# Projecting the dilated attention groups in token order instead of residue order, in a two-layer decoder trunk

## The chip, the cores and the metric

The kernel runs on one core of one Trainium2 chip. The metric is the device time of one execution in microseconds (us), as the median of several runs. Five engines work side by side, each through its own list of instructions in order: TensorE (PE; its weight loads are told apart as PEld) multiplies matrices, VectorE (DVE) and ScalarE (ACT) do elementwise work, GpSimd (POOL) does little here, and SyncE (SP) issues every DMA.

## The reference: what is computed

Two layers, each a token mixer and a feed-forward block over 512 tokens of 1024 channels. The part that the change touches is the dilated attention, branch A of the mixer:

```
for g, (window, dilation) in enumerate(((128, 1), (512, 4), (2048, 16))):
    q = apply_partial_rope(qkv_a[:, :, g, 0], cos, sin)
    k = apply_partial_rope(qkv_a[:, :, g, 1], cos, sin)
    o, lse = dilated_causal_attention(q, k, qkv_a[:, :, g, 2], window, dilation)
# alpha = softmax over the three groups of lse;  o_a = sum over groups of alpha * o
```

A query of a group with dilation d attends to keys whose token number has the same remainder modulo d. With 512 tokens and four heads per group, the groups with dilation 4 and 16 both live inside the four residue classes modulo 4, of 128 tokens each. Beside branch A there are a sparse attention with an indexer and a top-128 selection (B), a differential attention (C), sigmoid gates, and a gated convolutional feed-forward.

## The kernel before, in words

All matrix products are done in float32 as three products of a high and a low part (`mm3`, lines L88 to L90: hi*hi, hi*lo, lo*hi). The normalized input stands transposed in SBUF as `xh` and `xl` (128 channels on partitions, 8 channel blocks `KT`, 512 tokens). Weights come in from DRAM by SP into `wr` (two buffers) and are split into `wh` (a cast on ACT, L81) and `wl` (a subtraction on DVE, L82), five buffers each.

The mixer runs through the list `ORDER`: projection units A(g,p), where g is the group and p a pair of heads, the indexer I, then C and B units, and four branch stages (`ga`, `gc`, `gb`) that multiply the gates and the finished attention outputs. One projection unit (`proj_unit`) makes four token tiles of 128; each tile is 24 matmuls with 128 tokens of `xh` or `xl` as the stationary operand and 384 weight columns (q, k and v of two heads) as the moving one, into one of three PSUM banks `mm`. Then ACT copies q and k out (`qr`, L416), ACT and DVE split v into high and low parts straight from PSUM (L81, L82), DVE applies the rotary embedding, and after every second tile PE transposes q and k (L439) into a PSUM bank `tp`, from which ACT and DVE build the stacked operands `qkT` (`double_k`, L395 and L397; `stack_q`, L388 to L391): six reads by ACT and six by DVE for each two tiles.

The groups g = 1 and g = 2 are projected in residue order: tile t takes tokens t, t+4, t+8, ..., so that `xtile` gives a slice with a step of four floats. These are four units in each layer: A(1,0), A(2,0), A(1,1), A(2,1). Every other unit takes 128 neighbouring tokens:

```
if perm:
    return lambda k: (xh[:, k, t::4], xl[:, k, t::4])
return lambda k: (xh[:, k, t * P:(t + 1) * P], xl[:, k, t * P:(t + 1) * P])
```

The attention itself is cut into chains (scores, transposed probabilities, product with v), which `slot()` starts one by one between tiles and branch steps; `later(f, n)` puts f off by n slots. The joint output of groups 1 and 2 goes through DRAM once (`ascr`, L579 and L581) to come back in token order. The order of the instructions on each engine is set by the scheduler of the framework when the program is built, from its own estimates; on the chip each engine then works through its list.

Of the kernel before, what the change touches and what calls it, by code (L numbers as in the profile page):

```python
# [17 lines left out]
P = 128  # L18
# [19 lines left out]
TWO_PI = [6.28125, 0.0019350051879882812, 3.019813448190689e-07]  # L38
TWO_PI_REST = 1.0253376273028358e-11
MAGIC = 12582912.0  # L40
SBUF_SLOTS = dict(u=10, qk=4, v=4, wr=2, wh=5, wl=5, sm=4, pt=4, qr=2, th=3, s=24, s1=2, md=4, wi=1, lp=1, q0=2, cw=1)
PSUM_BANKS = dict(mm=3, sc=2, tp=2, pv=1)

ORDER = [("A", 0, 0), "I", ("A", 1, 0), ("A", 2, 0), ("A", 0, 1), ("A", 1, 1), ("A", 2, 1), ("C", 0), ("C", 1),
# [5 lines left out]
def tile_trunk(ctx, tc, x, positions, w_in, w_br_a, w_br_b, w_br_c, w_out, lam_q1, lam_k1, lam_q2, lam_k2,  # L50
# [10 lines left out]
    def alloc(shape, dtype, tag):  # L61
        uid[0] += 1
        return sb.tile(shape, dtype, tag=tag, name=f"{tag}{uid[0]}", bufs=SBUF_SLOTS[tag])

# [186 lines left out]
    first += [pre_norm(xts[t], t, g_first, xts[t]) for t in range(2, NT)]  # L251
    pos_n = alloc([4, P], I32, "pt")
    nc.sync.dma_start(pos_n, positions[0].rearrange("(t p) -> t p", p=P))
    pos_p = alloc([P, 4], I32, "pt")
    nc.sync.dma_start(pos_p, positions[0].rearrange("(p r) -> p r", r=4))

    cmask = cp.tile([P, S], BF16, name="cmask")
    nc.gpsimd.memset(cmask, 0.0)
# [19 lines left out]

    posf_n = alloc([4, P], F32, "pt")
    nc.vector.tensor_copy(posf_n, pos_n)  # L280
    posf = alloc([P, 8], F32, "pt")
    tpos = palloc("tp")
    nc.tensor.transpose(tpos[:, 0:4], posf_n, ident[0:4, 0:4])
    nc.vector.tensor_copy(posf[:, 0:4], tpos[:, 0:4])
    nc.vector.tensor_copy(posf[:, 4:8], pos_p)
    ang = alloc([P, 8, 8], F32, "th")
    for f in range(8):
        nc.vector.tensor_scalar(ang[:, :, f], posf, INV_FREQ[f], None, op0=ALU.mult)
    rn = alloc([P, 8, 8], F32, "sm")
    rh = alloc([P, 8, 8], F32, "sm")  # L290
    rl = alloc([P, 8, 8], F32, "sm")

    def round_(dst, src, mul):
        nc.vector.tensor_scalar(dst, src, mul, None, op0=ALU.mult)
# [8 lines left out]
        nc.vector.scalar_tensor_tensor(ang, rl, -c, ang, op0=ALU.mult, op1=ALU.add)  # L303
    nc.vector.scalar_tensor_tensor(ang, rn, -TWO_PI_REST, ang, op0=ALU.mult, op1=ALU.add)
    nc.vector.tensor_scalar(ang, ang, 3.1415925, -3.1415925, op0=ALU.min, op1=ALU.max)
    cc = cp.tile([P, 8, 2, 8], F32, name="cc")
    sn = cp.tile([P, 8, 8], F32, name="sn")
    nsn = cp.tile([P, 8, 8], F32, name="nsn")
    nc.scalar.activation(sn, ang, AF.Sin)
    nc.vector.tensor_scalar(nsn, sn, -1.0, None, op0=ALU.mult)  # L310
    nc.vector.scalar_tensor_tensor(ang, ang, -1.0, ang, op0=ALU.mult, op1=ALU.max)
# [15 lines left out]
    def later(f, lag=1):  # L327
        pending.append([lag, f])
# [40 lines left out]
    def heads(a):  # L369
        return a.rearrange("p (h d) -> p h d", d=HD)  # L370

    def xtile(t, perm):
        if perm:
            return lambda k: (xh[:, k, t::4], xl[:, k, t::4])
        return lambda k: (xh[:, k, t * P:(t + 1) * P], xl[:, k, t * P:(t + 1) * P])

    def proj_tile(units, t, perm, n):
        acc = palloc("mm")
        xs = xtile(t, perm)
        for k in range(KT):  # L380
            hi, lo = units[k // 2]
            mm3(acc[:, 0:n], xs(k), (hi[:, k % 2], lo[:, k % 2]), k == 0, k == KT - 1)
        return acc


# [16 lines left out]

    def proj_unit(l, u, perm, nh, idx=None):

        keys = [(l, u, kk) for kk in range(4)]
        n = sum(w for _, w in unit_cols[u])
        dv = P // nh
        qkT = alloc([P, 6, S], F32R, "qk")
        v = alloc([P, NT, nh, 2, dv], F32R, "v")
        raws = []  # L410
        for t in range(NT):
            units = w_get(keys)
            acc = proj_tile(units, t, perm, n)
            w_ahead(2)
            qr = alloc([P, 384], F32, "qr")
            nc.scalar.copy(qr[:, 0:256], acc[:, 0:256])  # L416
            vv = acc[:, 256:384].rearrange("p (h d) -> p h d", h=nh)
            split(v[:, t, :, 0, :], v[:, t, :, 1, :], vv)
            nh_r = 4
            if idx is not None:  # L420
                nc.scalar.copy(qr[:, 256:320], acc[:, 384:448])
                nc.scalar.activation(idx["w"][:, t, :], acc[:, 448:456], AF.Copy, scale=float(8 ** -0.5))
                nh_r = 5
            rope(heads(qr[:, 0:nh_r * HD]), nh_r, t + (4 if perm else 0))
            if idx is not None:
                nc.vector.tensor_copy(qr[:, 320:384], qr[:, 256:320])
            raws.append(qr)

            def tk(t=t, qr=qr):
                tp = palloc("tp")  # L430
                nc.tensor.transpose(tp[:, 0:P], qr[:, 256:384], ident)
                c = slice(t * P, (t + 1) * P)
                split(idx["k"][:, 0, c], idx["k"][:, 1, c], tp[:, 0:P])

            def tqk(j=t // 2):
                tp = palloc("tp")
                for i in range(2):
                    for w in range(2):
                        nc.tensor.transpose(tp[:, (2 * w + i) * P:(2 * w + i + 1) * P],  # L439
                                            raws[2 * j + i][:, w * P:(w + 1) * P], ident)  # L440
                c = slice(j * 256, (j + 1) * 256)
                for h in range(2):
                    double_k(qkT[:, 2 + 2 * h, c], qkT[:, 3 + 2 * h, c], tp[:, 256:512], HALF[h])
                stack_q(qkT[:, 0, c], qkT[:, 1, c], tp[:, 0:256])

            if idx is not None:
                later(tk, 2)
            if t % 2 == 1:
                later(tqk, 2)
# [244 lines left out]
    def index_q(l, qi):  # L694
        keys = [(l, "I", kk) for kk in range(4)]
        for t in range(1, NT):
            units = w_get(keys)
            acc = proj_tile(units, t, False, 512)
            w_ahead(2)
            qr = alloc([P, 512], F32, "sm")  # L700
            nc.scalar.copy(qr, acc)
            rope(heads(qr), 8, t)

            def go(t=t, qr=qr):
                tp = palloc("tp")
# [98 lines left out]
    for l in range(DEPTH):  # L804
# [25 lines left out]
        for u in ORDER:  # L830
            if u[0] in BRANCH:
                gi = BRANCH[u[0]]
                last_br = u == ORDER[-1]
                if not ys:
                    ys = [alloc([P, 2, S], F32, "u") for _ in range(4)]
                while None in (oTa, oTb, oTc)[gi] or (last_br and (pending or chains or fly != [None, None])):
                    slot()
                if last_br:
                    yT = []
                    for c in range(8):  # L840
                        if c % 3 == 0:
                            yq = alloc([P, 6, S], F32R, "qk")
                        yT.append((yq[:, 2 * (c % 3)], yq[:, 2 * (c % 3) + 1]))
                for c in branch(l, gi, u[1], u[2], (oTa, oTb, oTc)[gi], ys, gi == 0):
                    if last_br:
                        split(yT[c][0], yT[c][1], ys[c // 2][:, c % 2], scale=0.5)
                continue
            if u == "I":
                index_q(l, qi)
                later(lambda: index_scores(qi, idx["k"], idx["w"], masks), 3)  # L850
            elif u[0] == "A":
                g, p = u[1], u[2]
                qkT, v = proj_unit(l, u, g > 0, 2, idx if u == ("A", 0, 0) else None)
                if g == 0:
                    res = {}
                    a1[p, 0] = res
                    later(lambda qkT=qkT, v=v, res=res: chains_a0(qkT, v, res), 3)
                elif g == 1:
                    a1[p, 1] = (qkT, v)
                else:  # L860
                    def go(p=p, qkT=qkT, v=v):
                        def fin(opn):
                            on = combine_a(a1[p, 0]["o0"], a1[p, 0]["md"], opn)
                            to_oT(on, oTa, p, lag=4)
                        chains_a12(*a1[p, 1], qkT, v, a_scr[l][p], fin)
                    later(go, 3)
            elif u[0] == "C":
                qkT, v = proj_unit(l, u, False, 1)
                later(lambda qkT=qkT, v=v, h=u[1]: chains_c(qkT, v, nlam, subg, oTc, h), 3)
            else:  # L870
                qkT, v = proj_unit(l, u, False, 2)
                later(lambda qkT=qkT, v=v, p=u[1]: chains_b(qkT, v, masks, oTb, p), 3)
            slot()

# [154 lines left out]
```

## Time and profile before

| | |
|---|---|
| median of 3 runs | 1914.39 us (1914.26 to 1916.31) |
| profiled execution | 1916.77 us, of which 1915.0 us lie between its first and last instruction |
| PE busy | 1884.9 us, 98% of the span |
| PE weight loads busy | 1659.3 us, 87% |
| DVE busy | 1241.3 us, 65% |
| ACT busy | 853.4 us, 45% |
| DMA | 181.08 MB, mean 95 GB/s |

Busy times are shares of the whole span and average over stages with different limits. A matmul's busy time overlaps that of the next, since matmuls are pipelined; how fast they follow one another is read from the difference of two start times.

### The profile page before, as it was taken

The page shows a single profiled execution, that of the slowest core. Times are in us where ns is not written, and L with a number is a line of the kernel's source. Part 1 is how long each engine was busy: PE and PEld are TensorE (multiplying, and loading weights), DVE is VectorE, ACT ScalarE, POOL GpSimd, SP SyncE. Part 2 cuts the span into 40 slices and gives each one's busy share as a digit, 9 for nine tenths or more (in the row PEclk, how much of TensorE's full clock was granted, in tenths as well). Part 3 has the DMA queues.
Part 4 walks back from the last instruction along what each step waited for, and adds up shares of the span by engine and source line. Part 5 has one row for each costly group of instructions (what it writes and reads, how often), then busy time and mean ns, then how long its engine had stood idle before and what let it go on. Part 6 is the DMA issues. An engine that isn't in the chain of part 4 may idle for free.

```text
span 1915.0 us, 26238 instructions
## 1 busy us (share of the span) xinstructions
PE 1884.9 (98%) x9565; PEld 1659.3 (87%) x9565; DVE 1241.3 (65%) x2695; ACT 853.4 (45%) x1692; POOL 28.8 (2%) x53
## 2 busy tenths in 40 slices
PE   7999999999999999999999999899999999999998
PEld 6999988898889888888889999799888898888886
DVE  6687898774446766642377879887645466666332
ACT  5555554463334544432264646544533354444221
POOL 0000000000000000000000000000000000000000
PEclk9999999999999999999999999999999999999999
DMA  5322231333334323323432222322323433333241
GB/s 150 79 55 61 67 100 42 80 108 88 100 125 129 115 88 106 92 99 124 127 111 56 67 63 70 88 64 68 112 72 106 144 120 107 93 99 100 99 144 66
DMA packets 259564, 181.08 MB, mean 95 GB/s; under 512 B 14214, under 2 KB 233706, under 8 KB 259434
## 3 DMA queue, kind: packets, MB, share of 16 engines
q1 hardware_dynamic: 259434, 179.40, 32.1%
q8 instruction: 75, 1.23, 0.3%
q14 instruction: 55, 0.45, 0.1%
HBM read 169.89 MB, written 9.47 MB: 94 GB/s over the span
## 4 chain that ended last, share of the span: by engine, by line
PE 91%; DVE 4%; DMA 2%; ACT 1%; issue 1%; SPq 0%; POOL 0%; DVEq 0%; POOLq 0%; ACTq 0%
PE mm L88 21%; PE mm L89 21%; PE mm L90 21%; PE sc L89 4%; PE sc L90 4%; PE sc L88 4%; PE pv L89 2%; PE pv L88 2%; PE pv L90 2%; PE pv L477 2%; PE sc L400 2%; PE sc L401 2%; PE tp L466 2%; PE tp L439 1%; PE pv L478 1%
## 5 line engine op out<-in xcount | busy, mean ns | idle before, releaser
L82 DVE TENSOR_TENSOR wl<-wr,wh 128x1024 fp32r<-128x1024 f32 (+2 forms) x314 | 359.0, 1146 | 347.7 <-ACT wh L81 346.7
L81 ACT CAST wh<-wr 128x1024 fp32r<-128x1024 f32 (+2 forms) x314 | 310.2, 989 | 441.6 <-PE mm L90 137.3
L88 PE MATMUL mm<-xh,wh 128*128 128x512 f32 (+1 forms) x784 | 297.5, 380 | 2.2 <-DVE v L82 0.9
L90 PE MATMUL mm<-wh,xl 128*128 128x384 f32 (+2 forms) x816 | 299.4, 369 | 0.0
L88 PE MATMUL mm<-wh,xh 128*128 128x384 f32 (+2 forms) x816 | 298.6, 369 | 0.8 <-ACT xh L81 0.7
L89 PE MATMUL mm<-wl,xh 128*128 128x384 f32 (+2 forms) x816 | 297.6, 366 | 1.1 <-DVE wl L82 1.1
L89 PE MATMUL mm<-xl,wh 128*128 128x512 f32 (+1 forms) x784 | 296.5, 378 | 0.0
L90 PE MATMUL mm<-xh,wl 128*128 128x512 f32 (+1 forms) x784 | 295.9, 377 | 0.5 <-DVE wl L82 0.5
L89 PEld LDWEIGHTS mm<-wl,xh 128*128 128x128 f32 x816 | 189.9, 233 | 5.6 <-DVE wl L82 1.9
L88 PEld LDWEIGHTS mm<-wh,xh 128*128 128x128 f32 x816 | 189.6, 233 | 5.7 <-ACT xh L81 1.9
L90 PEld LDWEIGHTS mm<-wh,xl 128*128 128x128 f32 x816 | 189.7, 233 | 3.7 <-DVE xl L82 0.3
L88 PEld LDWEIGHTS mm<-xh,wh 128*128 128x128 f32 x784 | 147.9, 189 | 29.3 <-DVE v L82 1.3
L90 PEld LDWEIGHTS mm<-xh,wl 128*128 128x128 f32 x784 | 147.8, 189 | 27.6 <-DVE wl L82 0.7
L89 PEld LDWEIGHTS mm<-xl,wh 128*128 128x128 f32 x784 | 147.7, 188 | 26.2 <-DVE xl L82 0.4
L90 PE MATMUL sc<-xh,wl 128*128 128x512 f32 (+1 forms) x272 | 99.2, 365 | 0.0
L89 PE MATMUL sc<-xl,wh 128*128 128x512 f32 (+1 forms) x272 | 99.0, 364 | 0.0
L88 PE MATMUL sc<-xh,wh 128*128 128x512 f32 (+1 forms) x272 | 98.8, 364 | 0.0
L395 ACT CAST qk<-tp 64x256 fp32r<-64x256 f32 x192 | 70.6, 367 | 39.0 <-DVE qk L397 22.3
L397 DVE TENSOR_TENSOR qk<-tp,qk 64x256 fp32r<-64x256 f32 x192 | 80.7, 420 | 8.5 <-ACT qk L395 5.7
L89 PE MATMUL mm<-wl,qk 128*128 128x512 f32 x216 | 85.8, 397 | 0.0
L88 PE MATMUL mm<-wh,qk 128*128 128x512 f32 x216 | 85.4, 395 | 0.0
L90 PE MATMUL mm<-wh,qk 128*128 128x512 f32 x216 | 84.9, 395 | 0.0
(261 smaller groups left out, 3341.9 us busy)
## 6 DMA issues: line engine op xcount, KB each, us to landing
wr<-in_w_ffn_up_dram SPq DMA_DIRECT2D x176, 256.0 KB, 3.4
wr<-in_w_in_dram SPq DMA_DIRECT2D x282, 128.0 KB, 2.4
wr<-in_w_in_dram SPq DMA_DIRECT2D x56, 512.0 KB, 3.8
wr<-in_w_ffn_down_dram SPq DMA_DIRECT2D x44, 512.0 KB, 3.6
wr<-in_w_out_dram SPq DMA_DIRECT2D x16, 512.0 KB, 3.6
xd<-u SPq DMA_DIRECT2D x12, 512.0 KB, 2.6
u<-xd SPq DMA_DIRECT2D x12, 512.0 KB, 5.4
u<-in_x_dram SPq DMA_DIRECT2D x8, 512.0 KB, 5.1
```

Of the source, the lines that this page charges most:

```text
L81: nc.scalar.copy(hi, src)
L82: nc.vector.tensor_tensor(lo, src, hi.bitcast(F32), op=ALU.subtract)
L88: nc.tensor.matmul(dst, a[0], b[0], start=start, stop=False)
L89: nc.tensor.matmul(dst, a[0], b[1], start=False, stop=False)
L90: nc.tensor.matmul(dst, a[1], b[0], start=False, stop=stop)
L395: nc.scalar.copy(kh[o], src[r])
L397: nc.vector.tensor_tensor(kl[o], src[r], kh[r].bitcast(F32), op=ALU.subtract)
L400: nc.tensor.matmul(dst, q, kh, start=True, stop=False)
L401: nc.tensor.matmul(dst, q, kl, start=False, stop=True)
L439: nc.tensor.transpose(tp[:, (2 * w + i) * P:(2 * w + i + 1) * P], raws[2 * j + i][:, w * P:(w + 1) * P], ident)
L466: nc.tensor.transpose(tp[:, b * P:(b + 1) * P], e[:, b * P:(b + 1) * P], ident)
L477: nc.tensor.matmul(dst, pT[0][:, c], v, start=i == 0, stop=False)
```

## The change

Groups 1 and 2 are projected in token order like all other units, and put in residue order afterwards. For q and k this happens where ACT and DVE read the transposes out of PSUM: they read with a step of four floats, and write runs of 64 tokens into `qkT`. For v, ACT copies it out with q and k (384 columns in place of 256), SP writes it to DRAM tile by tile (`vscr`, 64 KB each), reads it back in residue order once per unit (`vr`, 256 KB), and one split per unit (`tv`) takes the place of four. `qr` has three buffers in place of two, and the second set of rotary tables, for the residue order, goes.

```diff
-SBUF_SLOTS = dict(u=10, qk=4, ..., qr=2, th=3, ...)
+SBUF_SLOTS = dict(u=10, qk=4, ..., qr=3, vr=1, th=3, ...)
...
+    v_scr = [[[dr.tile([S, P], F32, name=f"vscr{l}_{g}_{p}") for p in range(2)] for g in range(2)] for l in range(DEPTH)]
...
-    def xtile(t, perm):
-        if perm:
-            return lambda k: (xh[:, k, t::4], xl[:, k, t::4])
-        return lambda k: (xh[:, k, t * P:(t + 1) * P], xl[:, k, t * P:(t + 1) * P])
-    def proj_tile(units, t, perm, n):
+    def proj_tile(units, t, n):
...
+            mm3(acc[:, 0:n], (xh[:, k, ts], xl[:, k, ts]), (hi[:, k % 2], lo[:, k % 2]), k == 0, k == KT - 1)
...
-            nc.scalar.copy(qr[:, 0:256], acc[:, 0:256])
-            vv = acc[:, 256:384].rearrange("p (h d) -> p h d", h=nh)
-            split(v[:, t, :, 0, :], v[:, t, :, 1, :], vv)
+            nq = 384 if perm is not None else 256
+            nc.scalar.copy(qr[:, 0:nq], acc[:, 0:nq])
+            if perm is not None:
+                nc.sync.dma_start(perm[t * P:(t + 1) * P, :], qr[:, 256:384])
+            else:
+                vv = acc[:, 256:384].rearrange("p (h d) -> p h d", h=nh)
+                split(v[:, t, :, 0, :], v[:, t, :, 1, :], vv)
...
-            rope(heads(qr[:, 0:nh_r * HD]), nh_r, t + (4 if perm else 0))
+            rope(heads(qr[:, 0:nh_r * HD]), nh_r, t)
...
-                c = slice(j * 256, (j + 1) * 256)
+                if perm is not None:
+                    at = lambda i: qkT[:, i].rearrange("p (r i) -> p r i", r=NT)[:, :, j * 64:(j + 1) * 64]
+                    qt, kt = (tp[:, c:c + 256].rearrange("p (i r) -> p r i", r=NT) for c in (0, 256))
+                else:
+                    at = lambda i: qkT[:, i, j * 256:(j + 1) * 256]
+                    qt, kt = tp[:, 0:256], tp[:, 256:512]
                 for h in range(2):
-                    double_k(qkT[:, 2 + 2 * h, c], qkT[:, 3 + 2 * h, c], tp[:, 256:512], HALF[h])
-                stack_q(qkT[:, 0, c], qkT[:, 1, c], tp[:, 0:256])
+                    double_k(at(2 + 2 * h), at(3 + 2 * h), kt, HALF[h])
+                stack_q(at(0), at(1), qt)
...
+        if perm is not None:
+            vr = alloc([P, NT, P], F32, "vr")
+            nc.sync.dma_start(vr, perm.rearrange("(i r) c -> i r c", r=NT))
+
+            def tv():
+                vv = vr.rearrange("p t (h d) -> p t h d", h=nh)
+                split(v[:, :, :, 0, :], v[:, :, :, 1, :], vv)
+            later(tv, 2)
         return qkT, v
```

The scheduler orders the whole program anew, so small shifts are found all along. Two places matter below.

On ACT, around the border between the units A(1,0) and A(2,0) of layer 0, the kernel before has these rows. `mm_1034` is the last tile of A(1,0), `mm_1108` the first of A(2,0), and `v_761` the v of A(1,0):

```order
L416 COPY qr_1075<-mm_1034 128x256
L81 CAST v_761<-mm_1034 128x2x64
L81 CAST wh_648<-wr_647 128x768
L723 ACTIVATE sm_1088<-sc_1085 128x256
L723 ACTIVATE sm_1094<-sc_1091 128x256
L81 CAST wh_710<-wr_709 128x768
L395 CAST qk_760<-tp_1159 64x256 x2
L416 COPY qr_1149<-mm_1108 128x256
```

The changed kernel has these; `mm_1036` is the last tile of A(1,0), `mm_1111` the first of A(2,0), `v_766` the v of A(1,0), and `vr_1086` what comes back from DRAM:

```order
L411 COPY qr_1077<-mm_1036 128x384
L734 ACTIVATE sm_1091<-sc_1088 128x256
L734 ACTIVATE sm_1097<-sc_1094 128x256
L381 CAST qk_765<-tp_989 64x4x64
L382 CAST qk_765<-tp_989 64x4x64
L81 CAST pt_1023<-tp_1018 128x512
L81 CAST wh_715<-wr_714 128x768
L734 ACTIVATE sm_1183<-sc_1180 128x256
L81 CAST v_766<-vr_1086 128x8x64
L411 COPY qr_1152<-mm_1111 128x384
L734 ACTIVATE sm_1189<-sc_1186 128x256
L388 CAST qk_765<-tp_1161 64x4x64 x4
```

The cast of v has moved from right behind its tile's copy to right ahead of the copy of the next unit's first tile, and it now waits for a DMA; the reads of `tp` have the same number of elements in four runs.

On SP, at the border between A(1,1) and A(2,1) of layer 0, the kernel before issues:

```order
L579 DMA ascr_0_238<-u_1545 128x528
L126 DMA wr_1216<-in_w_in_dram 128x2x128 x3
L581 DMA u_2072<-ascr_0_238 128x4x132
L126 DMA wr_1224<-in_w_in_dram 128x2x128 x3
L126 DMA wr_1282<-in_w_in_dram 128x2x128 x3
```

The changed kernel issues the following; `qr_1822` to `qr_2135` are the four tiles of A(1,1), `wr_1220` and `wr_1228` the first two weight blocks of C(0):

```order
L413 DMA vscr_0_1_240<-qr_1822 128x128
L413 DMA vscr_0_1_240<-qr_1937 128x128
L413 DMA vscr_0_1_240<-qr_2020 128x128
L126 DMA wr_1144<-in_w_in_dram 128x2x128 x3
L126 DMA wr_1220<-in_w_in_dram 128x2x128 x3
L413 DMA vscr_0_1_240<-qr_2135 128x128
L590 DMA ascr_0_235<-u_1550 128x528
L457 DMA vr_2144<-vscr_0_1_240 128x512
L592 DMA u_2074<-ascr_0_235 128x4x132
L126 DMA wr_1228<-in_w_in_dram 128x2x128 x3
```

Five DMAs per unit have come into SP's list, and the weight blocks behind them are issued only when these have been.

## Rows read from the trace of the kernel before

**Rows 1.** Section 1 of the page: engine, busy us (share of the span), number of instructions.

```profile
PE 1884.9 (98%) x9565; PEld 1659.3 (87%) x9565; DVE 1241.3 (65%) x2695; ACT 853.4 (45%) x1692; POOL 28.8 (2%) x53
```

**Rows 2.** Section 4 of the page: the chain of work that ended last, shares of the span by engine.

```profile
PE 91%; DVE 4%; DMA 2%; ACT 1%; issue 1%; SPq 0%; POOL 0%; DVEq 0%; POOLq 0%; ACTq 0%
```

**Rows 3.** Busy time by stretch. The columns are: the stretch, its length, and the busy time (number of instructions) of PE, PEld, DVE, ACT and POOL, then the granted clock of TensorE, the busy share of the DMA engines, and GB/s. Layer 0: the units A(1,0) to A(2,1); C(0) to C(2); the first branch stage. Then the same three of layer 1.

```profile
59.00:201.00 142.00, 142.00 (x758) 140.95 (x756) 110.78 (x329) 75.08 (x194) 0.00 (x0) 1.00 0.26 63
201.00:270.00 69.00, 69.00 (x449) 68.33 (x448) 63.43 (x204) 42.57 (x113) 0.00 (x0) 1.00 0.31 78
270.00:315.00 45.00, 40.96 (x195) 33.93 (x194) 40.58 (x110) 23.18 (x58) 2.08 (x2) 0.92 0.27 71
1004.00:1146.00 142.00, 142.00 (x756) 140.92 (x754) 110.36 (x330) 74.97 (x194) 0.00 (x0) 1.00 0.24 61
1146.00:1214.00 68.00, 68.00 (x441) 67.25 (x440) 60.67 (x199) 40.86 (x111) 0.00 (x0) 1.00 0.30 78
1214.00:1264.00 50.00, 42.76 (x205) 35.58 (x204) 44.78 (x120) 24.22 (x59) 2.03 (x2) 0.93 0.24 64
```

**Rows 4.** Groups of PE weight loads between 90 and 116 us (unit A(2,0), stationary operand with a step of four floats): line, engine, operation, tiles, shape, count | busy us, mean ns of one | idle before.

```profile
L89 PEld LDWEIGHTS mm<-wl,xh 128*128 128x128 f32 x32 | 10.5, 329 | 0.0
L90 PEld LDWEIGHTS mm<-wh,xl 128*128 128x128 f32 x32 | 10.5, 329 | 0.0
L88 PEld LDWEIGHTS mm<-wh,xh 128*128 128x128 f32 x31 | 10.2, 328 | 0.0
```

**Rows 5.** The same groups between 201.2 and 221.8 us (unit C(0), stationary operand of neighbouring tokens).

```profile
L89 PEld LDWEIGHTS mm<-wl,xh 128*128 128x128 f32 x32 | 6.0, 189 | 0.0
L90 PEld LDWEIGHTS mm<-wh,xl 128*128 128x128 f32 x32 | 6.0, 188 | 0.0
L88 PEld LDWEIGHTS mm<-wh,xh 128*128 128x128 f32 x31 | 5.8, 188 | 0.0
```

**Rows 6.** PE's matmuls in order of time in unit A(2,0): start us, us, engine, line, operation. The first and the last of 13 that follow one another with nothing between.

```profile
104.66 0.40 PE L89 MATMUL mm<-wl,xh 128*128 128x384 f32 x1
104.90 0.40 PE L90 MATMUL mm<-wh,xl 128*128 128x384 f32 x1
...
107.46 0.40 PE L89 MATMUL mm<-wl,xh 128*128 128x384 f32 x1
```

**Rows 7.** The same in unit C(0): the first and the last of nine.

```profile
207.26 0.33 PE L89 MATMUL mm<-wl,xh 128*128 128x384 f32 x1
207.43 0.33 PE L90 MATMUL mm<-wh,xl 128*128 128x384 f32 x1
...
208.64 0.34 PE L88 MATMUL mm<-wh,xh 128*128 128x384 f32 x1
```

**Rows 8.** Groups of DVE instructions over the whole span, shapes kept apart (columns as in rows 4, idle time with what ended it).

```profile
L397 DVE TENSOR_TENSOR qk<-tp,qk 64x256 fp32r<-64x256 f32 x192 | 80.7, 420 | 8.5 <-ACT qk L395 5.7
L82 DVE TENSOR_TENSOR pt<-tp,pt 128x512 fp32r<-128x512 f32 x40 | 27.5, 687 | 21.1 <-ACT pt L81 20.7
L82 DVE TENSOR_TENSOR v<-mm,v 128x128 fp32r<-128x128 f32 x96 | 27.3, 285 | 2.0 <-ACT v L81 1.4
L514 DVE TENSOR_REDUCE th<-pv 128x256 f32<-128x512 f32 x24 | 16.5, 687 | 19.6 <-PE pv L478 19.4
L82 DVE TENSOR_TENSOR v<-sm,v 128x512 fp32r<-128x512 f32 x8 | 5.5, 692 | 5.5 <-ACT v L81 5.5
```

**Rows 9.** Groups of ACT instructions over the whole span, shapes kept apart.

```profile
L395 ACT CAST qk<-tp 64x256 fp32r<-64x256 f32 x192 | 70.6, 367 | 39.0 <-DVE qk L397 22.3 <-PE tp L439 14.6
L416 ACT COPY qr<-mm 128x256 f32<-128x256 f32 x96 | 35.8, 373 | 80.7 <-PE mm L90 51.4 <-PE tp L439 21.7 <-issue 6.7
L81 ACT CAST v<-mm 128x128 fp32r<-128x128 f32 x96 | 26.1, 272 | 0.0
L81 ACT CAST v<-sm 128x512 fp32r<-128x512 f32 x8 | 5.0, 620 | 22.3 <-DVE sm L958 22.3
L701 ACT COPY sm<-mm 128x512 f32<-128x512 f32 x6 | 3.5, 588 | 5.7 <-PE mm L90 5.6
```

**Rows 10.** DMA issues by line: what is moved, issuing engine, count, KB each, median us from issue to landing.

```profile
wr<-in_w_in_dram SPq DMA_DIRECT2D x282, 128.0 KB, 2.4
ascr<-u SPq DMA_DIRECT2D x4, 264.0 KB, 2.7
u<-ascr SPq DMA_DIRECT2D x4, 264.0 KB, 3.0
```

**Rows 11.** SP's DMA issues in order of time around the round trip of `ascr`: start us, us taken on SP.

```profile
170.93 0.47 SPq L579 DMA_DIRECT2D ascr<-u  x1
172.44 1.41 SPq L126 DMA_DIRECT2D wr<-in_w_in_dram  x3
173.89 1.52 SPq L581 DMA_DIRECT2D u<-ascr  x1
```

**Rows 12.** PE in order of time in the first branch stage of layer 0: the last matmul of a gate and the first that reads `u`, the finished output of branch A.

```profile
277.34 0.40 PE L90 MATMUL mm<-xh,wl 128*128 128x512 f32 x1
280.87 0.71 PE L88 MATMUL mm<-u,wh 128*128 128x512 f32 x1 [3.13 <-DVE v L82]
```

More of the change, by code (lines that the diff above doesn't have):

```diff
@@ L40 @@
 MAGIC = 12582912.0
-SBUF_SLOTS = dict(u=10, qk=4, v=4, wr=2, wh=5, wl=5, sm=4, pt=4, qr=2, th=3, s=24, s1=2, md=4, wi=1, lp=1, q0=2, cw=1)
+SBUF_SLOTS = dict(u=10, qk=4, v=4, wr=2, wh=5, wl=5, sm=4, pt=4, qr=3, vr=1, th=3, s=24, s1=2, md=4, wi=1, lp=1, q0=2, cw=1)
 PSUM_BANKS = dict(mm=3, sc=2, tp=2, pv=1)
@@ L253, in tile_trunk @@
     nc.sync.dma_start(pos_n, positions[0].rearrange("(t p) -> t p", p=P))
-    pos_p = alloc([P, 4], I32, "pt")
-    nc.sync.dma_start(pos_p, positions[0].rearrange("(p r) -> p r", r=4))
     cmask = cp.tile([P, S], BF16, name="cmask")
@@ L280, in tile_trunk @@
     nc.vector.tensor_copy(posf_n, pos_n)
-    posf = alloc([P, 8], F32, "pt")
+    posf = alloc([P, 4], F32, "pt")
     tpos = palloc("tp")
     nc.tensor.transpose(tpos[:, 0:4], posf_n, ident[0:4, 0:4])
-    nc.vector.tensor_copy(posf[:, 0:4], tpos[:, 0:4])
-    nc.vector.tensor_copy(posf[:, 4:8], pos_p)
-    ang = alloc([P, 8, 8], F32, "th")
+    nc.vector.tensor_copy(posf, tpos[:, 0:4])
+    ang = alloc([P, NT, 8], F32, "th")
     for f in range(8):
         nc.vector.tensor_scalar(ang[:, :, f], posf, INV_FREQ[f], None, op0=ALU.mult)
-    rn = alloc([P, 8, 8], F32, "sm")
-    rh = alloc([P, 8, 8], F32, "sm")
-    rl = alloc([P, 8, 8], F32, "sm")
+    rn = alloc([P, NT, 8], F32, "sm")
+    rh = alloc([P, NT, 8], F32, "sm")
+    rl = alloc([P, NT, 8], F32, "sm")
     def round_(dst, src, mul):
@@ L305, in tile_trunk @@
     nc.vector.tensor_scalar(ang, ang, 3.1415925, -3.1415925, op0=ALU.min, op1=ALU.max)
-    cc = cp.tile([P, 8, 2, 8], F32, name="cc")
-    sn = cp.tile([P, 8, 8], F32, name="sn")
-    nsn = cp.tile([P, 8, 8], F32, name="nsn")
+    cc = cp.tile([P, NT, 2, 8], F32, name="cc")
+    sn = cp.tile([P, NT, 8], F32, name="sn")
+    nsn = cp.tile([P, NT, 8], F32, name="nsn")
     nc.scalar.activation(sn, ang, AF.Sin)
@@ L370, in heads @@
         return a.rearrange("p (h d) -> p h d", d=HD)
-    def xtile(t, perm):
-        if perm:
-            return lambda k: (xh[:, k, t::4], xl[:, k, t::4])
-        return lambda k: (xh[:, k, t * P:(t + 1) * P], xl[:, k, t * P:(t + 1) * P])
-    def proj_tile(units, t, perm, n):
+    def proj_tile(units, t, n):
         acc = palloc("mm")
-        xs = xtile(t, perm)
+        ts = slice(t * P, (t + 1) * P)
         for k in range(KT):
             hi, lo = units[k // 2]
-            mm3(acc[:, 0:n], xs(k), (hi[:, k % 2], lo[:, k % 2]), k == 0, k == KT - 1)
+            mm3(acc[:, 0:n], (xh[:, k, ts], xl[:, k, ts]), (hi[:, k % 2], lo[:, k % 2]), k == 0, k == KT - 1)
         return acc
@@ L412, in proj_unit @@
             units = w_get(keys)
-            acc = proj_tile(units, t, perm, n)
+            acc = proj_tile(units, t, n)
             w_ahead(2)
             qr = alloc([P, 384], F32, "qr")
-            nc.scalar.copy(qr[:, 0:256], acc[:, 0:256])
-            vv = acc[:, 256:384].rearrange("p (h d) -> p h d", h=nh)
-            split(v[:, t, :, 0, :], v[:, t, :, 1, :], vv)
+            nq = 384 if perm is not None else 256
[5 more added lines that the diff above has]
+                split(v[:, t, :, 0, :], v[:, t, :, 1, :], vv)
             nh_r = 4
@@ L697, in index_q @@
             units = w_get(keys)
-            acc = proj_tile(units, t, False, 512)
+            acc = proj_tile(units, t, 512)
             w_ahead(2)
@@ L852, in tile_trunk @@
                 g, p = u[1], u[2]
-                qkT, v = proj_unit(l, u, g > 0, 2, idx if u == ("A", 0, 0) else None)
+                qkT, v = proj_unit(l, u, v_scr[l][g - 1][p] if g > 0 else None, 2, idx if u == ("A", 0, 0) else None)
                 if g == 0:
@@ L867, in tile_trunk @@
             elif u[0] == "C":
-                qkT, v = proj_unit(l, u, False, 1)
+                qkT, v = proj_unit(l, u, None, 1)
                 later(lambda qkT=qkT, v=v, h=u[1]: chains_c(qkT, v, nlam, subg, oTc, h), 3)
             else:
-                qkT, v = proj_unit(l, u, False, 2)
+                qkT, v = proj_unit(l, u, None, 2)
                 later(lambda qkT=qkT, v=v, p=u[1]: chains_b(qkT, v, masks, oTb, p), 3)
```

## The prediction

> **What bounds the kernel now.** I read the summary of busy time first: PE is busy 98% of the span, DVE 65%, ACT 45% [rows 1]. The chain that ended last agrees: 91% of it is PE [rows 2]. Then I cut the span into stretches, because the change sits in one of them per layer. From 59 to 201 us (the four dilated units of layer 0) PE is busy 142.00 of 142 us while DVE has 110.78 and ACT 75.08; layer 1 repeats this within half a microsecond [rows 3]. So there PE alone sets the time, at a granted clock of 1.00, the 2.4 GHz level.
>
> A busy PE is not a PE at its peak, so the next look is at how fast its matmuls follow one another. In A(2,0), 13 matmuls of 384 columns start over 2.80 us, so 12 steps of 233.3 ns [rows 6]; in C(0), nine start over 1.38 us, 8 steps of 172.5 ns [rows 7]. The shape is the same and so is the clock. What differs is the weight load: 329 ns where the stationary slice steps by four floats, 188 ns where it is contiguous [rows 4, 5]. The load of the next matmul runs under the present one, so of the 141 ns only 60.8 show per step: PE here waits for its own weight loads.
>
> **Removed: the stepped weight loads.** Four units per layer, two layers, four tiles, 8 channel blocks, 3 products: 8 x 4 x 24 = 768 matmuls. 768 x 60.8 ns = 46.7 us, half of it in each layer: the stage of 142 us becomes 118.7. The time is PE's own, on the path, at full clock.
>
> The Trainium skill, "SBUF — State Buffer", section "Door 1: The DMA port swizzle", says that SBUF has lines of 16 bytes, that accesses crossing to a new line pay, and that a stride of four fp32 is still free. By that last sentence these loads would cost nothing extra and the change would leave 1914; rows 4 and 5 disagree, so it is only a rival.
>
> **Added to the reads of `tp`.** Per unit 12 reads by ACT (367 ns of 64x256) and 12 by DVE (420 ns) [rows 8, 9] become stepped reads of PSUM. For DVE a near row exists: the `TENSOR_REDUCE` of `pv` jumps 64 or 128 floats at every element it reads and takes 687 ns for 512, as a contiguous read of `tp` does (687) [rows 8]. So I cost DVE's reads at nothing. For ACT no row reads PSUM in steps. Lower end: nothing (a gain has no ground, since the element count stays). Upper end: what the step costs a weight load, 141 ns for 128 elements, so 282 ns for 256 and 13.5 us per layer for 48 reads. ACT would then be at 75.1 + 13.5 = 88.6 of 118.7 us, still with a quarter of the stage free. I take nothing, since DVE's row is the nearest thing, and keep the upper end for both engines.
>
> **v.** Per unit DVE loses four subtractions of 285 ns and gains one of 692: -0.45 us. ACT loses four casts of 272 and gains one of 620; its copies grow from 373 towards 588 ns (the 512-column copy), an estimate of 480 for 384 columns: -1.09 + 0.62 + 4 x 0.107 = -0.04 us [rows 8, 9]. Nothing on the path. A gain is possible, since the bank `mm` is now freed by ACT's copy alone, but PE is never idle in these stages and so does not wait for a bank.
>
> **The round trip and its queue.** Each unit adds five DMAs on SP. One issue takes 0.47 us on SP in the trace [rows 11], so 20 in a layer are 9.4 us of a queue that mostly waits for buffers. The path of v is: ACT's copy of the last tile, issue 0.47, landing 2.7, issue 0.47 again, landing 3.0 [rows 10, 11]: 6.6 us, with larger transfers than the new ones of 64 and 256 KB, so rather less. The bytes, 4 MB over the kernel, are nothing against queues that are 26% busy [rows 3].
>
> Behind this wait stands, on ACT, the copy of the next unit's first tile (the order above). That tile needs 24 x 172.5 ns = 4.1 us of PE and some score matmuls between, so ACT may be held 1 to 2 us at each unit. Who waits for ACT then is PE, through the banks `mm`: there are three, so two further tiles (8.3 us) must run before PE stops. ACT has 43 us free per layer even after the shortening (118.7 - 75.1). Cost: nothing, covered by the banks; without that cover, up to 2 us in each of 8 units.
>
> On SP, the weight blocks behind the read of `vr` are `wr_1228` at the one border shown, the second block of the unit after next, which is needed a whole unit (about 20 us, as C(0) takes [rows 5]) later. A load lands in 2.4 us [rows 10]. Nothing.
>
> The third `qr` buffer lifts some waits of ACT for transposes: 21.7 us of ACT's idle time ended there [rows 9]. ACT is not the bound; I count nothing.
>
> **Who is late next.** DVE. Its work per layer is 110.8 - 4 x 0.45 = 109.0 us in a stage of 118.7: 92%. That is exactly what the stretch 201 to 270 has (63.43 of 69, 92%), and PE is busy 69.00 of 69 there [rows 3]. So the stage can run at PE's speed with DVE so full. What shrinks is the reserve with which DVE enters C(0) to C(2), and behind these the first branch stage is where PE does stop today: 3.1 us idle before the first matmul that reads `u`, and over the stretch 4.0 us idle in layer 0 and 7.2 in layer 1, with the granted clock down to 0.92 and 0.93 [rows 3, 12], so part of it ran at the 1.2 GHz level. I add 3 us there for a later DVE, about a quarter of the 11.3 idle now; the ends are minus 6 (half of it goes, since the schedule is redone) and plus 11 (it doubles).
>
> **Sum.** -46.7 + 3 = -43.7 us. Against the profiled execution, 1916.8 with 1.8 outside its span, that is 1873.1; the median of the runs is 2.4 lower, so 1870.7. I predict **1871**.
>
> **Rivals.**
>
> *Stepped reads of PSUM are slow, and DVE becomes the bound.* With 282 ns more on 48 reads per layer DVE has 109.0 + 13.5 = 122.5 us, more than the 118.7 of PE. If DVE could be full the stage would take 122.5 (39 us saved over both layers, 1875); at the 92% at which the rows show PE undisturbed it takes 133 (18 saved, 1896). For it: the step did cost PE's loads. Against it: the `TENSOR_REDUCE` row. About 1886 in the middle.
>
> The Trainium skill, "PSUM — Partial Sum Buffer", section "Specifications (TRN2)", speaks for this rival: PSUM's lines are 8 bytes and any non-contiguous pattern slows matmuls significantly. It speaks of matmuls; for reads by ACT and DVE the reduce row disagrees for DVE, and no row shows ACT.
>
> *The stop in the branch stage doubles.* DVE's delay is carried through C(0) to C(2), which have only 8% of DVE free to recover it, and 11.3 us of idle PE become 22.6: 1914.4 - 46.7 + 11.3 = 1879, or some microseconds more if the lower clock also lasts longer: 1879 to 1888.
>
> *Slower: ACT is held by the wait for `vr`.* If the data come so late that the banks run out, PE stops in all 8 units. Cover is three tiles, 12.4 us; the gain per unit is 46.7 / 8 = 5.8 us. So it decides from 18.2 us between the copy and the landing, against the 6.6 worked out; for instance if SP stood long before the write of `ascr` that now precedes the read of `vr`. At 19.5 us the price is 7.1 per unit, and the time 1914.4 - 46.7 + 56.8 = 1924.
>
> *The change does not do what it says.* If the 233 ns came from something else in these units, the steps stay and the time is 1914. Against it: same tile, shape and clock in rows 4 to 7, and only the slice differs.
>
> **Chances.** The forecast, with a time of 1862 to 1878: 0.66. Slow reads of PSUM: 0.18. The longer stop: 0.09. Held ACT, slower: 0.04. No effect: 0.03. The low end of the range is 1914.4 - 46.7 - 6 = 1862. The high end, 1888, takes in the longer stop and half of the slow reads; left out are the other half, the slower case and no effect, 0.16. Faster by over 0.2% (3.8 us, about what a measurement of this kernel can tell): 0.66 + 0.18 + 0.09 = 0.93. Slower 0.04, within 0.2% 0.03.
>
> **What the profile after would show.** Right: weight loads of `xh` and `xl` at 188 ns in all units, steps of about 173 ns, the four-unit stages near 119 us with PE busy throughout and DVE at 92%; DVE's reads of `tp` in four runs of 64 at 420 ns; the wait of ACT for `vr` at 2 us or less, with no idle PE after it. Wrong, if those reads take 500 ns or more on either engine, if PE's steps fall to 173 ns but gaps open between tiles with DVE full, or if the branch stages that take 45 and 50 us today grow by more than 3 us each.

## The result

| | before | changed kernel |
|---|---|---|
| median | 1915.35 us (4 runs) | 1873.43 us (1872.52 to 1874.62, 4 runs) |
| ratio, 95% interval | | 0.9781 (0.9764 to 0.9798) |
| span of the profiled execution | 1915.0 us | 1870.7 us |

The changed kernel is 41.9 us faster; 43.7 had been forecast, and the range was 1862 to 1888. First the summary of busy time of the changed kernel (as in [rows 1]) and its chain by engine (as in [rows 2]):

```profile
PE 1836.4 (98%) x9565; PEld 1606.0 (86%) x9565; DVE 1233.6 (66%) x2670; ACT 852.5 (46%) x1668; POOL 29.8 (2%) x53
```

```profile
PE 80%; DVE 11%; DMA 3%; issue 2%; ACT 2%; SPq 1%; POOL 0%; DVEq 0%; POOLq 0%; ACTq 0%
```

PE has lost 48.5 us of busy time with the same number of matmuls, DVE (7.7 us less) and ACT have about kept theirs, and the chain now passes through DVE for 11% of the span where it was 4%.

Weight loads of the changed kernel in A(2,0) (82 to 103 us, as in [rows 4]), and there the first and the last of eight matmuls that follow one another (as in [rows 6]):

```profile
L89 PEld LDWEIGHTS mm<-wl,xh 128*128 128x128 f32 x31 | 5.8, 188 | 0.0
L90 PEld LDWEIGHTS mm<-wh,xl 128*128 128x128 f32 x31 | 5.8, 188 | 0.0
L88 PEld LDWEIGHTS mm<-wh,xh 128*128 128x128 f32 x31 | 5.8, 188 | 0.0
```

```profile
91.72 0.34 PE L90 MATMUL mm<-wh,xl 128*128 128x384 f32 x1
...
92.93 0.34 PE L88 MATMUL mm<-wh,xh 128*128 128x384 f32 x1
```

A load takes 188 ns, as in the other units, and a step 1.21 us / 7 = 172.9 ns where it was 233.3.

Busy time by stretch of the changed kernel, with the columns of [rows 3]: per layer, the dilated units (with A(0,1), which stands between them), then C(0) up to the first matmul of C(3), with the first branch stage in it. Under it the second kind of stretch for the kernel before, cut in the same way:

```profile
59.10:177.50 118.40, 118.23 (x755) 115.51 (x754) 103.39 (x311) 76.62 (x188) 0.00 (x0) 1.00 0.33 84
177.50:293.90 116.40, 109.22 (x640) 100.58 (x640) 104.14 (x308) 65.34 (x168) 1.02 (x1) 0.99 0.31 79
983.30:1103.70 120.40, 119.40 (x766) 116.87 (x765) 105.95 (x317) 75.85 (x186) 0.00 (x0) 1.00 0.31 82
1103.70:1219.50 115.80, 108.37 (x630) 99.56 (x629) 103.45 (x305) 63.74 (x165) 1.02 (x1) 0.99 0.29 80
```

```profile
201.00:314.90 113.90, 109.86 (x642) 102.16 (x641) 103.91 (x313) 65.65 (x171) 2.08 (x2) 0.97 0.29 75
1146.20:1263.50 117.30, 110.06 (x640) 102.16 (x640) 104.75 (x311) 64.39 (x169) 2.03 (x2) 0.97 0.27 72
```

The dilated stages went from 142 us to 118.4 and 120.4 (in layer 1 with 766 matmuls in the stretch where it had 756). PE, never idle there before, now stands 0.2 and 1.0 us. The stretch behind it has 7.2 and 7.4 us of idle PE, where it had 4.0 and 7.2.

The 1.0 us in layer 1 stands ahead of one matmul of A(1,1). The profile's chain that leads to it (start us, us, what; the pieces in a row):

```profile
1049.45 0.87 DVE wl L82
1050.32 0.15 DVE qr L365
1050.47 0.25 SPq L126
1050.72 0.04 issue
1050.76 1.27 SPq L126
1052.03 0.04 issue
1052.07 2.39 DMA wr<-in_w_in_dram
1054.56 0.84 ACT wh L81
1055.40 0.04 issue
1055.44 0.45 PE mm L88
```

A weight block was issued only behind DVE's split of an earlier one, and PE then stood for its load and its cast. So DVE's lateness reached PE here by way of the weight buffers, not by way of `vr`.

The groups of the changed kernel that read the transposes, copy q, k and v out and split v (as in [rows 8, 9]), the DMA issues of the round trip (as in [rows 10]), and the total of one wait (engine and line, what it waited for: us, times, longest):

```profile
L388 ACT CAST qk<-tp 64x256 fp32r<-64x256 f32 x192 | 70.2, 366 | 33.3 <-DVE qk L390 26.1 <-PE tp L437 5.3
L411 ACT COPY qr<-mm 128x384 f32<-128x384 f32 x32 | 15.2, 476 | 9.6 <-PE mm L90 7.7 <-issue 1.7
L390 DVE TENSOR_TENSOR qk<-tp,qk 64x256 fp32r<-64x256 f32 x192 | 80.6, 420 | 7.7 <-ACT qk L388 4.8
L82 DVE TENSOR_TENSOR v<-vr,v 128x512 fp32r<-128x512 f32 x8 | 5.5, 685 | 4.0 <-ACT v L81 4.0
```

```profile
vscr<-qr SPq DMA_DIRECT2D x32, 64.0 KB, 1.5
vr<-vscr SPq DMA_DIRECT2D x8, 256.0 KB, 2.8
```

```profile
ACT v L81 <- DMA vr<-vscr: 7.3, 5, 2.3
```

A third of the reads of `tp` are now stepped, and the means are those of before, 366 and 420 ns; the 64 stepped ones of each of these two lines, taken alone, have means of 365 and 420. The round trip holds ACT five times in eight, 7.3 us in all.

### The profile page after: what moved, and what is told of

It is laid out like the page before. It is cut to its first block, busy times and chain, and to the rows that moved or that the text cites. A ratio compares the mean times of both kernels' runs of the same rounds, so it can differ in the third digit from the quotient of the medians.

```text
span 1870.7 us, 26241 instructions
## 1 busy us (share of the span) xinstructions
PE 1836.4 (98%) x9565; PEld 1606.0 (86%) x9565; DVE 1233.6 (66%) x2670; ACT 852.5 (46%) x1668; POOL 29.8 (2%) x53
## 4 chain that ended last, share of the span: by engine, by line
PE 80%; DVE 11%; DMA 3%; issue 2%; ACT 2%; SPq 1%; POOL 0%; DVEq 0%; POOLq 0%; ACTq 0%
PE mm L88 18%; PE mm L89 18%; PE mm L90 18%; PE sc L89 4%; PE sc L88 4%; PE sc L90 4%; PE pv L89 2%; PE pv L88 2%; PE pv L90 2%; DVE wl L82 1%; DVE qk L390 1%; DMA wr<-in_w_in_dram 1%; PE pv L488 1%; PE tp L477 1%; DVE u L746 1%
## 5 line engine op out<-in xcount | busy, mean ns | idle before, releaser
L89 PE MATMUL mm<-wl,xh 128*128 128x384 f32 (+2 forms) x816 | 282.8, 347 | 1.1 <-DVE wl L82 1.1
L88 PE MATMUL mm<-wh,xh 128*128 128x384 f32 (+2 forms) x816 | 281.1, 349 | 2.2 <-ACT wh L81 1.0
L90 PE MATMUL mm<-wh,xl 128*128 128x384 f32 (+2 forms) x816 | 282.6, 347 | 0.0
L88 PEld LDWEIGHTS mm<-wh,xh 128*128 128x128 f32 x816 | 153.9, 189 | 8.1 <-ACT xh L81 2.0
L89 PEld LDWEIGHTS mm<-wl,xh 128*128 128x128 f32 x816 | 154.4, 189 | 6.2 <-DVE wl L82 2.5
L90 PEld LDWEIGHTS mm<-wh,xl 128*128 128x128 f32 x816 | 154.3, 189 | 3.9 <-DVE s L226 0.3
```

The source lines that it names most:

```text
L88: nc.tensor.matmul(dst, a[0], b[0], start=start, stop=False)
L89: nc.tensor.matmul(dst, a[0], b[1], start=False, stop=False)
L90: nc.tensor.matmul(dst, a[1], b[0], start=False, stop=stop)
```

## The experiments

**The stepped weight loads alone, taken away from the kernel before** (every engine's order as before):

```diff
-            return lambda k: (xh[:, k, t::4], xl[:, k, t::4])
+            return lambda k: (xh[:, k, t * P:(t + 1) * P], xl[:, k, t * P:(t + 1) * P])
```

> The kernel before with one line changed: the dilated units take 128 neighbouring tokens as stationary operand; nothing is put in residue order, so groups 1 and 2 attend over the wrong keys. The instructions stand in the same order on every engine as before. My theory (the step of the weight loads is the whole gain): weight loads of 188 ns everywhere, 46.7 us less, and up to 6 given back in the branch stage: 1867 to 1875. Rival (a good part of the gain comes from the new schedule, the third qr buffer or the freed banks): above 1885.

Measured: 1867.28 us, ratio 0.9751 (0.9737 to 0.9766), 47.0 us less than the kernel before on the same chip (1914.27). Its stretches, cut as above:

```profile
59.50:176.80 117.30, 117.30 (x755) 115.66 (x754) 105.49 (x321) 73.69 (x194) 0.00 (x0) 1.00 0.30 73
176.80:291.60 114.80, 111.16 (x643) 102.38 (x642) 107.66 (x322) 65.67 (x171) 2.08 (x2) 0.97 0.30 78
980.70:1098.20 117.50, 117.50 (x756) 115.80 (x755) 107.13 (x327) 73.61 (x192) 0.00 (x0) 1.00 0.28 72
1098.20:1214.10 115.90, 110.88 (x640) 101.29 (x639) 106.34 (x317) 64.92 (x170) 2.03 (x2) 0.97 0.28 76
```

PE is busy throughout the dilated stages with DVE at 105.49 of 117.30, 90%. The step of the loads is the whole gain, and in this order nothing is given back: 114.8 + 115.9 us behind the dilated units, 113.9 + 117.3 before.

**The stepped loads alone, put back into the changed kernel** (every engine's order as in the changed kernel):

```diff
-        ts = slice(t * P, (t + 1) * P)
+        ts = slice(t, S, 4) if stepped else slice(t * P, (t + 1) * P)
```

> The changed kernel, with the step of four floats put back into the weight loads of the dilated units alone (residue order is then applied twice, so groups 1 and 2 are wrong); order on every engine as in the changed kernel. My theory: 329 ns per load, 233 ns per step again, 768 x 60.8 ns = 46.7 us, less what the branch stage no longer loses: 1912 to 1920, as the kernel before. Rival (the new schedule or the v path brings a part of the gain by itself): under 1905.

Measured: 1914.05 us, ratio 0.9998 (0.9988 to 1.0007). So the round trip, the stepped reads, the third `qr` buffer and the new order together cost nothing that can be measured while PE is slowed by its loads. Its stretches:

```profile
57.70:199.60 141.90, 141.90 (x755) 140.91 (x754) 108.80 (x318) 77.74 (x188) 0.00 (x0) 1.00 0.28 73
199.60:313.60 114.00, 108.06 (x641) 100.73 (x641) 100.59 (x300) 65.64 (x168) 1.02 (x1) 0.99 0.30 78
1002.90:1146.00 143.10, 143.10 (x766) 142.11 (x765) 110.51 (x322) 77.96 (x187) 0.00 (x0) 1.00 0.28 75
1146.00:1259.90 113.90, 107.33 (x630) 99.60 (x630) 100.76 (x301) 63.57 (x165) 1.02 (x1) 0.99 0.27 75
```

Against this run, in the same order, the changed kernel gains 23.5 and 22.7 us in the dilated units, together 46.2, and loses 2.4 and 1.9 in the stretches behind them. This is the term that the prediction called a later DVE, 4.3 us of it: 2.1 us are more idle PE (5.9 to 7.2 and 6.6 to 7.4), the rest is longer busy time of PE, whose cause is not traced.

**The parts that were added, taken out one at a time.** q and k read without a step:

```diff
-                if perm is not None:
+                if False:
                     at = lambda i: qkT[:, i].rearrange("p (r i) -> p r i", r=NT)[:, :, j * 64:(j + 1) * 64]
```

> The changed kernel, q and k read from PSUM without a step and written in token order (groups 1 and 2 attend over the wrong keys). My theory (stepped reads of PSUM cost nothing on either engine): 1873 within 4 us of the scheduler's shifts. Rival (the reads cost a part of the 282 ns each): 1860 to 1867.

Measured: 1868.65 us, ratio 0.9766 (0.9749 to 0.9782). v split straight from PSUM:

```diff
-            nq = 384 if perm is not None else 256
+            nq = 256
...
-            if perm is not None:
-                nc.sync.dma_start(perm[t * P:(t + 1) * P, :], qr[:, 256:384])
-            else:
+            if True:
```

> The changed kernel without the round trip of v: v is split straight from PSUM in token order as in the other units, 40 DMAs less, q and k still in residue order (groups 1 and 2 weigh the wrong v). My theory (the round trip is hidden): 1873 within 4 us, with no wait of ACT for vr. Rival (the 7.3 us that ACT waits for vr, and SP's five issues per unit, reach PE): 1864 to 1868.

Measured: 1871.87 us, ratio 0.9777 (0.9762 to 0.9791). Neither is apart from the changed kernel by more than the intervals. The first, 4.8 us below by the medians, lies between the two expectations; but the reads themselves take 366 and 420 ns with and without the step, so if it is faster it is not for them. Both edits made the scheduler lay out the whole program anew, and a difference of this size cannot be told from that.

**A new order without the new work**: the first experiment with the third `qr` buffer.

```diff
-SBUF_SLOTS = dict(u=10, ..., qr=2, th=3, ...)
+SBUF_SLOTS = dict(u=10, ..., qr=3, th=3, ...)
```

> The kernel before with contiguous slices in the dilated units, as e1_contig (1867.3), and with three qr buffers in place of two, which makes the scheduler order the whole program anew; no round trip, no stepped reads (groups 1 and 2 attend over the wrong keys). Theory A (the 6 us by which the changed kernel is above e1_contig come from the new order of the instructions): 1869 to 1875 and idle PE moved to other places. Theory B (they come from the round trip and the reads of the transposes): 1865 to 1869, as e1_contig.

Measured: 1868.09 us, ratio 0.9762 (0.9747 to 0.9776). This is theory B's number; that interval also touches the one of the changed kernel, so how the 6 us between 1867.3 and 1873.4 divide stays open.

**A longer path of v**: sent through DRAM twice.

```diff
             nc.sync.dma_start(vr, perm.rearrange("(i r) c -> i r c", r=NT))
+            nc.sync.dma_start(perm.rearrange("(i r) c -> i r c", r=NT), vr)
+            vr = alloc([P, NT, P], F32, "vr")
+            nc.sync.dma_start(vr, perm.rearrange("(i r) c -> i r c", r=NT))
```

> The changed kernel with v sent through DRAM twice (written back from vr and read again), so that its path is longer by a write and a read, about 6 us by the rows of ascr; the scheduler puts the cast of v one tile later at most borders. Theory (the path is hidden up to about 12 us): 1873 within 4 us. Rival (ACT's wait reaches PE): 4 us or more at each of 8 units, above 1890.

Measured: 1870.59 us, ratio 0.9774 (0.9760 to 0.9789). ACT was held for `vr` eight times, 13.8 us in all and 2.7 at most, where it was five times, 7.3 and 2.3, and the longer path costs nothing. With the cast of v a tile later it is no test of ACT held at the old place.

**The step by itself.** The four dilated units with steps of 2, 3, 4 and 8 floats:

```diff
-            return lambda k: (xh[:, k, t::4], xl[:, k, t::4])
+            return lambda k: (fl(xh)[:, at(k)], fl(xl)[:, at(k)])
...
+                {(1, 0): 2, (2, 0): 3, (1, 1): 4, (2, 1): 8}.get((g, p), 0)
```

> The kernel before, with another step of the stationary slice in each dilated unit: 2 floats in A(1,0), 3 in A(2,0), 4 in A(1,1) as before, 8 in A(2,1) (the slices then hold the wrong tokens). It measures the price of a step by itself. If the price comes with fewer than two elements per 16 bytes: 188 ns at 2, about 330 at 4 and at 8, and something between at 3. If it grows with the step: about 235, 280, 329 and over 400.

One execution was taken (1893.63 us), so each step has one unit behind it in the lines shown. One line of weight loads for each, in this order (62 to 82, 85 to 104, 130 to 160, 163 to 189 us):

```profile
L89 PEld LDWEIGHTS mm<-wl,xh 128*128 128x128 f32 x26 | 5.1, 195 | 0.0
L89 PEld LDWEIGHTS mm<-wl,xh 128*128 128x128 f32 x29 | 7.4, 254 | 0.0
L89 PEld LDWEIGHTS mm<-wl,xh 128*128 128x128 f32 x29 | 9.5, 327 | 0.1
L89 PEld LDWEIGHTS mm<-wl,xh 128*128 128x128 f32 x29 | 9.8, 338 | 0.0
```

And the first and the last of 12 successive matmuls at a step of 3, and of 16 at a step of 8:

```profile
94.98 0.34 PE L88 MATMUL mm<-wh,xh 128*128 128x384 f32 x1
96.92 0.34 PE L90 MATMUL mm<-wh,xl 128*128 128x384 f32 x1
```

```profile
174.35 0.40 PE L90 MATMUL mm<-wh,xl 128*128 128x384 f32 x1
177.99 0.40 PE L90 MATMUL mm<-wh,xl 128*128 128x384 f32 x1
```

195, 254, 327 and 338 ns: the price goes with elements per 16 bytes and is nearly flat from one on. The steps are 1.94 / 11 = 176 ns and 3.64 / 15 = 243 ns: of the 65 ns that a step of 3 adds to a load, 4 are seen, of the 150 at 8, 70. As an estimate, if the step from one matmul to the next follows the load nanosecond for nanosecond as it does between 329 and 338 ns (233.3 and 243), it comes down to 173 at a load of 338 - 70 = 268 ns: up to about there a load is hidden under 384 columns, but for the 4 ns seen at 254.

**Is it DVE that stops PE behind the dilated units?** First a shorter top-k selection:

```diff
-        for rnd in range(16):
+        for rnd in range(12):
```

> The changed kernel with 12 in place of 16 rounds of the top-k selection (96 in place of 128 keys are found, so branch B is wrong). It takes work from DVE alone: three tiles of 512, 384 and 256 columns, 1.45 + 1.18 + 0.92 us per round, 14 us per layer. Theory (the idle PE left in the branch stages comes from a full DVE): PE's idle of about 6 us per layer falls below 3, 1863 to 1869. Rival (it is the length of a chain of dependent steps): 1871 to 1875.

Measured: 1878.32 us, ratio 0.9812 (0.9795 to 0.9828): if anything slower, a miss for both. The selection is paced by slots, four thirds of a step in each, so it ended sooner without being thinner where PE stops. So next the pace:

```diff
-            tick[0] += 4
+            tick[0] += 3
```

> The changed kernel with the top-k selection started at one step per slot in place of four thirds, so that DVE's work of the units C(0) to C(2) is put off until C(3) and the second branch stage; nothing is left out. (In e7_topk12 the selection only ended sooner: DVE's share fell to 0.69 between C(3) and B(0), and stayed at 0.89 and 0.90 where PE stops.) Theory (the idle PE of 7.2 and 7.4 us comes from a full DVE): idle falls by 2 us or more per layer, 1866 to 1871. Rival (a chain of dependent steps, whatever DVE's load): 1871 to 1876.

Measured: 1865.42 us, ratio 0.9749 (0.9732 to 0.9765), the lowest of all, 0.6 us under the expected range, with nothing left out. The stretches:

```profile
58.50:175.70 117.20, 117.20 (x756) 115.72 (x755) 101.87 (x304) 76.68 (x188) 0.00 (x0) 1.00 0.33 85
175.70:289.80 114.10, 108.32 (x641) 100.41 (x639) 99.88 (x300) 65.15 (x168) 2.03 (x2) 0.99 0.31 81
979.70:1096.90 117.20, 117.20 (x755) 115.58 (x754) 102.86 (x306) 75.24 (x184) 0.00 (x0) 1.00 0.32 85
1096.90:1210.70 113.80, 108.46 (x642) 100.52 (x641) 101.25 (x305) 66.87 (x172) 2.03 (x2) 0.99 0.30 81
```

PE is again busy throughout the dilated units, 117.2 us each; idle time behind them is 5.8 and 5.3 us, where it was 7.2 and 7.4. The idle fell by 1.4 and 2.1, where 2 or more had been expected per layer. Against the changed kernel the two intervals just meet (0.9765 and 0.9764). The same pace in the kernel before, with nothing else changed there:

```diff
-            tick[0] += 4
+            tick[0] += 3
```

> The kernel before with the slower top-k pace of e10_pace. Theory (the slower pace pays since the change made DVE scarce in the dilated units): these units take 142 us as before, only the stretch C(0) to C(3) can gain, 1909 to 1914. Rival (the pace is a better schedule with or without the change): the same 8 us as in the changed kernel, 1906.

Measured: 1916.48 us, ratio 1.0014 (1.0005 to 1.0024). This is a miss for both expectations: there it gains nothing and costs 1 to 5 us by its interval, so of these two kernels the slower pace pays only in the one whose dilated units run fast. Its stretches behind the dilated units:

```profile
202.20:316.00 113.80, 109.51 (x640) 101.86 (x639) 95.42 (x293) 64.96 (x170) 2.03 (x2) 0.97 0.29 75
1148.00:1262.00 114.00, 109.14 (x644) 101.78 (x644) 98.16 (x301) 66.57 (x173) 2.03 (x2) 0.99 0.28 77
```

In layer 0 DVE went from 91% (103.91 of 113.90 us) to 84%, and the idle time of PE stayed: 4.0 us before, 4.3 here. In layer 1 it fell from 7.2 to 4.9. And half the pace, in the changed kernel:

```diff
-            tick[0] += 4
+            tick[0] += 2
```

> The changed kernel with two thirds of a top-k step per slot, half the pace of the changed kernel; what is left of the selection then runs in one piece ahead of the B chains. Theory (DVE's load before C(3) is what costs): less idle before C(3) than with e10_pace, but a stop ahead of B of some microseconds: 1862 to 1870. Rival (e10_pace gained by the new order alone): above 1870.

Measured: 1894.71 us, ratio 0.9901 (0.9886 to 0.9916). Its stretch behind the dilated units of layer 0, and the stop that it gets instead, in order of time on PE:

```profile
178.00:287.70 109.70, 106.66 (x629) 99.39 (x629) 92.14 (x281) 63.91 (x166) 2.03 (x2) 0.98 0.32 84
```

```profile
417.41 0.47 PE L477 MATMUL tp<-ident,sm 128*128 128x128 f32 x1 [15.50 <-ACT sm L472]
```

With DVE at 92.14 of 109.70, 84%, the stretch takes 6.7 us less than in the changed kernel (11 of its matmuls now stand in the dilated units; the two stages together take 6.6 less), and idle falls from 7.2 to 3.0. This fits a full DVE as what stops PE there, but does not show it: the order of the instructions is new here too, and over the runs DVE's share and PE's idle time do not go together. The first experiment has DVE at 107.66 of 114.80, 94%, and 3.6 us of idle PE; the kernel before at the slower pace has 84% and 4.3. What the traces show is that most of these waits end at a DVE instruction, 6.4 of the 7.2 us in layer 0 of the changed kernel. Whether it is late because DVE is full or because of the place of its work in DVE's list stays open. The rest of the selection then ran in one piece, and PE stood 15.5 us for it, and 14.2 in layer 1: the expectation had this stop, at far too small a price, and the time came out where the rival had it, above 1870. Last, other work taken from DVE, by giving it to GpSimd:

```diff
-        nc.vector.tensor_tensor(t2[:, 0:nh, 0:8], v[:, :, 8:16], ns_, op=ALU.mult)
-        nc.vector.tensor_tensor(t2[:, 0:nh, 8:16], v[:, :, 0:8], s_, op=ALU.mult)
+        nc.gpsimd.tensor_tensor(t2[:, 0:nh, 0:8], v[:, :, 8:16], ns_, op=ALU.mult)
+        nc.gpsimd.tensor_tensor(t2[:, 0:nh, 8:16], v[:, :, 0:8], s_, op=ALU.mult)
...
-                split(v[:, :, :, 0, :], v[:, :, :, 1, :], vv)
+                nc.scalar.copy(v[:, :, :, 0, :], vv)
+                nc.gpsimd.tensor_tensor(v[:, :, :, 1, :], vv, v[:, :, :, 0, :].bitcast(F32), op=ALU.subtract)
```

> The changed kernel with three pieces of DVE's work given to GpSimd, which is 2% busy: two of the four products of the rotary embedding (184 ns each on DVE, 88 of them and more in the other shapes) and the low part of v from vr (685 ns, 8 of them). About 40 us less on DVE over the kernel, some 15 of it before C(3) in each layer. Theory (DVE's fullness costs the changed kernel the microseconds above e1_contig): 1862 to 1870. Rival (GpSimd's longer latency or its share of the SBUF port with DVE eats it): 1873 or more.

Measured: 1869.96 us, ratio 0.9770 (0.9756 to 0.9785), the upper end of the theory's range and not to be told from the changed kernel. DVE's busy time fell by 15.7 us over the kernel (1233.6 to 1217.9) and not by 40, and behind the dilated units it stood at 91 and 89%, with 2.9 and 7.3 us of idle PE. So this is no test of a lighter DVE there.

## Why the prediction was right

- *What bounds it*: right. With every engine's order kept, the weight loads alone moved the time both ways: 47.0 us from the kernel before, and all of the gain back out of the changed one.
- *Their size*: 768 x 60.8 ns = 46.7 us forecast; 46.2 measured in the dilated units between the changed kernel and the one with stepped loads, in the same order.
- *Stepped reads of PSUM*: costed at nothing, and nothing: 366 ns on ACT (367 before) and 420 on DVE. So the rival that took 282 ns more for each falls. The sentence of the Trainium skill that spoke for it ("PSUM — Partial Sum Buffer", section "Specifications (TRN2)") is about matmuls, and nothing of it is seen at these reads.
- *v and its copies*: 476 ns for the 384-column copy, 480 estimated; 685 for the subtraction, 692 taken.
- *The round trip*: hidden, as argued. ACT was held at most 2.3 us at a time, where 1 to 2 had been forecast, 7.3 in all, and the one stop of PE in the dilated units that is over 0.2 us does not lead back to it. Taking the trip out moved the median by 1.6 us, inside the intervals.
- *Who is late next*: DVE, at 87 and 88% in the dilated stages against 92% forecast: it did 103.4 and 106.0 us of work there, not 109. What is given back behind them is 4.3 us in the pair of kernels with one order, against 3, and about half of that is idle PE. Between the kernel before and the changed one it is 1.0 us, 2.5 more in layer 0 and 1.5 less in layer 1. That DVE's fullness is the reason was argued, and the runs leave it open. The end "it doubles" did not come.
- *The stage*: the 142 us that the prediction calls the four dilated units hold A(0,1) as well. The count of 768 matmuls does not include it, so the sum stands.
- *What the prediction did not see*: 1.0 us of idle PE inside the dilated units of layer 1, behind a weight block that came late. It had named gaps with DVE full as a sign of being wrong; one such gap came, of this size. The order that the scheduler finds may itself be worth some microseconds: with four rounds of the selection left out, the kernel took 4.9 us more by the medians. No run isolates this.

## What to carry to other kernels

Where PE is busy all the time, compare the start-to-start step of equal matmuls between stages: a slice with a step in the stationary operand can cost a quarter of the rate (here 233 ns per matmul in place of 173) while the busy share reads 100%. Reorder on the engines that read PSUM, where a step of four floats cost nothing here, and not on the way into the array. After a stage becomes shorter, look at what is paced by its steps on the next-fullest engine: here a slower pace of that work brought 8 us more by the medians, with intervals that just meet, and in the kernel before it brought nothing.

## What the runs showed of the hardware

A weight load of 128 float32 columns takes 188 ns in a row, 195 at a step of 2 floats, 254 at 3, 327 at 4 and 338 at 8. The Trainium skill, "SBUF — State Buffer", section "Door 1: The DMA port swizzle", says that two accesses to a 16-byte line are needed for full bandwidth; steps of 2 and 4 agree with that. Its next statement, that a stride of four fp32 is free, does not hold for these loads: 327 ns.

A read of PSUM at a step of four floats took ACT 365 and DVE 420 ns for 256 elements, as a contiguous one does. The Trainium skill, "PSUM — Partial Sum Buffer", section "Specifications (TRN2)", says that patterns that are not contiguous slow matmuls down. No run here writes PSUM in steps from PE, and for reads by these two engines nothing of it is seen.
